# Stick-breaking attention in a two-layer decoder trunk: suffix sums by scans along rows in place of triangular matmuls

## The chip, the cores and the metric

One Trainium2 chip, one of its cores. The metric is the device time of one execution in microseconds (us). Three executions of the kernel before took 1234.39, 1236.29 and 1236.81 us, median 1236.29.

## What is computed

A trunk of two layers on x (512 tokens of 1024 channels, float32). Layer 0 has HGRN2 recurrence and forgetting attention, layer 1 a Griffin recurrent branch and stick-breaking attention with 8 heads of 64; each layer ends in an output projection, layer norms and a SwiGLU block. The change is in the stick-breaking attention:

```
z = einsum('bqhd,bkhd->bhqk', q, k) * 64 ** -0.5      # per block of 128 queries
mask = kpos < qpos
log_one_minus = where(mask, log_sigmoid(-z), 0)
suffix = cumsum(log_one_minus, axis=keys, reverse=True) - log_one_minus
w = where(mask, exp(log_sigmoid(z) + suffix), 0)
out = einsum('bhqk,bkhd->bqhd', w, v)
```

With softplus(z) = max(z, 0) + log(1 + exp(-|z|)), which is -log_sigmoid(-z), the exponent of w for one query is z minus the sum of softplus over this key and all later ones below the diagonal.

## The kernel before, in words

Every large product runs on TensorE (PE) in float32r with both operands split into a high and a low part, so that one product is three matmuls (`mm3`, L256 to L258). Weights come in chunks of 128x1024: SP issues the DMA into `ws`, ScalarE (ACT) casts the high part `wh` (L245), VectorE (DVE) subtracts to get the low part `wl` (L246); five such pairs of buffers exist. A projection `proj` is 24 matmuls of 512 columns into one of two PSUM banks "g"; the next but one projection has to wait until the bank is read.

Layer 1 (`layer1`) runs `griffin`, then the values (`values`), then four head pairs `sb_pair(hp)`; after the fourth, the first half of the output projection (`out_rows(yc, S_WO1)`, PE tile `po`) is emitted, so that its matmuls can stand between those of the fourth pair. A scheduler orders each engine's instructions by priorities; the engines then run them strictly in that order.

One pair, step by step. `qk_pair` projects q and k (tile `pj`) and writes, per head e, the high half of 64 rows and the low half of 64 rows of one tile (`qk`), the rest of k in `kz` (ACT L727, L734; DVE L730, L735, L736). The second ACT copy of k is ordered behind the first DVE read of the same bank. `sb_pair` then has **keys on the partitions**: for each key block j the scores of all later queries, 512-128j columns, packed into five tiles of 512 columns a pair. Per tile:

- PE: two matmuls and a bf16 mask matmul per block (L931 to L933) into a bank "s"; ACT copies it to `z` in SBUF (L935).
- softplus: DVE clamps at 41 (L936), ACT exp and log (L937, L938), DVE max with z (L939). ACT casts the high part `sh` (L941), DVE makes the low part `sl` (L942).
- sums over keys: since keys lie on partitions, PE sums them, by a triangular matrix `ntri` within a block and by a matrix of -1 `none` for every later block, each for `sh` and `sl` (L953, tile `cu`).
- DVE adds `cu` to `z` (L955), ACT takes exp in place (L956).

The weights then stand as the product with v wants them (L964, 16 matmuls into `po`, ordered behind the last exp).

Of the kernel before, what the change touches and what calls it, by code (L numbers as in the profile page):

```python
# [56 lines left out]
class Trunk:  # L57
    def __init__(self, tc, ctx, ins, out):
        self.tc, self.nc, self.out = tc, tc.nc, out
        self.ins = ins  # L60

        self.cp = ctx.enter_context(tc.tile_pool(name="cp", bufs=1))
        tile_ = lambda n, shape, dt=F32: setattr(self, n, self.cp.tile(shape, dt, name=n))
        tile_("par", [P, NPP])

        tile_("fill", [P, 64])
# [7 lines left out]
        tile_("ntri", [P, P], F32R)  # L74
        tile_("none", [P, P], F32R)
# [110 lines left out]

    def constants(self):
        nc, ins, ph, cp = self.nc, self.ins, self.ph, self.cp
        cst = self.sb.tile([P, 4, P], F32, tag="gb", bufs=1, name="cst")
# [6 lines left out]
        cp_(self.ntri, cst[:, 3, :])  # L196
        nc.gpsimd.tensor_scalar(self.none, cst[:, 3, :], 0.0, -1.0, ALU.mult, ALU.add)
# [516 lines left out]
    def qk_pair(self, iq, ik, low, high=None):  # L714

        nc = self.nc
        hv = (slice(0, 64), slice(64, P))
        if self.qk4:  # L720
# [12 lines left out]
        for e, d in enumerate(hv):
            nc.scalar.copy(ks[e][d], kp[d])  # L734
            nc.vector.tensor_copy(ks[e][hv[1 - e]], kp[d])  # L735
            nc.vector.tensor_tensor(low[e][d], kp[d], ks[e][d].bitcast(F32), ALU.subtract)  # L736
        return qs, ks

# [85 lines left out]
    def griffin(self, xr):  # L824
# [27 lines left out]
        for i in range(2):  # L852
            nc.scalar.dma_start(gw[i], self.ins["gw"][i])
        st = []
        for j in range(4):
            ps = xr[j]
            xp = self.sb.tile([P, T], F32, tag="act", bufs=16, name=self.nm("xp"))
# [12 lines left out]
            ig = self.t2k("ig", tag="sh")  # L870
# [4 lines left out]
        gts = []  # L875
        for j in range(4):
            ps = self.proj(S_GR + j)
            g = self.t2k("gt", tag="sl")
            A(g, ps, AF.Gelu_apprx_tanh)
            gi = self.newest()  # L880
            gts.append(g)
# [4 lines left out]
        for j in range(4):  # L886
# [25 lines left out]
    def sb_pair(self, hp, v):  # L912
# [3 lines left out]
        yh, yl = self.act("yh"), self.act("yl")  # L916
        po = self.bank("ho", "po")

        tiles = (((0, 3, 384), (0, 1, 0)), ((1, 3, 384), (1, 1, 0)), ((0, 2, 0), (1, 2, 256)), ((0, 0, 0),), ((1, 0, 0),))
        sp = {}  # L920
        for parts in tiles:
            z, l = self.t2k("z", tag="z"), self.t2k("l", tag="l")
            for e in (0, 1):
                mine = [p for p in parts if p[0] == e]
                if not mine:
                    continue
                ps = self.bank("s", "z")
                for _, j, o in mine:
                    n = T - j * P
                    b = slice(j * P, j * P + P)  # L930
                    nc.tensor.matmul(ps[:, o:o + n], k[e][:, b], q[e][:, j * P:T], start=True, stop=False)  # L931
                    nc.tensor.matmul(ps[:, o:o + n], self.kz[e][:, b], q[e][:, j * P:T], start=False, stop=False)
                    nc.tensor.matmul(ps[:, o:o + P], self.identb, self.sbmask, start=False, stop=True)  # L933
                c = slice(min(p[2] for p in mine), max(p[2] + T - p[1] * P for p in mine))
                nc.scalar.copy(z[:, c], ps[:, c])  # L935
            nc.vector.tensor_scalar(l, z, EXP_MAX, None, ALU.min)  # L936
            A(l, l, AF.Exp)  # L937
            A(l, l, AF.Ln, bias=self.one)  # L938
            nc.vector.tensor_tensor(l, l, z, ALU.max)  # L939
            sh, sl = self.t2k("sh", dt=F32R, tag="sh"), self.t2k("sl", dt=F32R, tag="sl")  # L940
            nc.scalar.copy(sh, l)  # L941
            nc.vector.tensor_tensor(sl, l, sh.bitcast(F32), ALU.subtract)  # L942
            for e, j, o in parts:
                sp[e, j] = (sh, sl, o)
            sp[parts] = z
        for ti, parts in enumerate(tiles):
            z = sp[parts]
            ps = self.bank(("pt", "po")[ti % 2], "cu")
            lo = [(self.none, sp[e, i], o + (i - j) * P, T - i * P) for e, j, o in parts for i in range(j + 1, NTB)]
            mms = [(self.ntri, sp[parts[0][:2]][:2] + (0,), 0, T)] + lo  # L950
            for n, (w, (sh, sl, oi), c, m) in enumerate(mms):
                for x in (sh, sl):
                    nc.tensor.matmul(ps[:, c:c + m], w, x[:, oi:oi + m], start=n == 0 and x is sh,  # L953
                                     stop=n == len(mms) - 1 and x is sl)
            nc.vector.tensor_tensor(z, z, ps, ALU.add)  # L955
            A(z, z, AF.Exp)  # L956
            ex = self.newest()

        at = {(e, j): (sp[parts], o) for parts in tiles for e, j, o in parts}
        for j in range(NTB):  # L960
            for e in range(2):
                h = 2 * hp + e
                z, o = at[e, j]
                nc.tensor.matmul(po[64 * e:64 * e + 64, j * P:T], v[j][:, h * 64:h * 64 + 64], z[:, o:o + T - j * P],  # L964
                                 start=j == 0, stop=j == NTB - 1)
                if j == 0 and e == 0:
                    self.behind(self.newest(), ex)
        self.put(po, yh, yl)
        return yh, yl

    def layer1(self, xr):
# [19 lines left out]
def hybrid_trunk_kernel(ctx: ExitStack, tc: tile.TileContext, out, **ins):  # L991
# [9 lines left out]
    with t.phase("l1", v=4, qk=7, kz=2, z=6, l=4, sh=5, sl=5) as t.ph:  # L1001
# [39 lines left out]
def layout(inp):  # L1041
# [70 lines left out]
```

## Time and profile before

| | us |
|---|---|
| runs, median of three | 1236.29 |
| the profiled execution's own time | 1234.76 |
| its span in the trace | 1233.0 |
| PE busy | 1211.3 (98%) |
| DVE busy | 760.3 (62%) |
| ACT busy | 522.0 (42%) |

The chain of work that ended last lies on PE for 90% of the span. A PE matmul row of 512 columns is 0.39 us long though the next starts 0.23 us later: ends are modelled, rows overlap, and so a short pause doesn't show as idle time. The engines' clock row shows the share of full speed that PE was granted.

### The profile page before, as it was taken

The page shows a single profiled execution, that of the slowest core. Times are in us where ns is not written, and L with a number is a line of the kernel's source. Part 1 is how long each engine was busy: PE and PEld are TensorE (multiplying, and loading weights), DVE is VectorE, ACT ScalarE, POOL GpSimd, SP SyncE. Part 2 cuts the span into 40 slices and gives each one's busy share as a digit, 9 for nine tenths or more (in the row PEclk, how much of TensorE's full clock was granted, in tenths as well). Part 3 has the DMA queues.
Part 4 walks back from the last instruction along what each step waited for, and adds up shares of the span by engine and source line. Part 5 has one row for each costly group of instructions (what it writes and reads, how often), then busy time and mean ns, then how long its engine had stood idle before and what let it go on. Part 6 is the DMA issues. An engine that isn't in the chain of part 4 may idle for free.

```text
span 1233.0 us, 15454 instructions
## 1 busy us (share of the span) xinstructions
PE 1211.3 (98%) x6119; PEld 985.0 (80%) x6119; DVE 760.3 (62%) x1157; ACT 522.0 (42%) x794; POOL 55.3 (4%) x81
## 2 busy tenths in 40 slices
PE   9999999999999999999999999999999999999997
PEld 7787777679888888878879776777988888888886
DVE  7638789768345635564387597686844554456346
ACT  7447567533333333332323757683333333333220
POOL 2000000000001000100000000000000100010001
PEclk9999999999999999999999998999999999999999
DMA  6421211134536433742324231102454642364321
GB/s 243 154 71 51 85 53 52 59 113 142 200 94 111 137 103 87 118 136 87 103 88 135 69 88 49 42 28 86 153 191 101 103 140 99 92 114 137 103 69 69
DMA packets 38727, 128.03 MB, mean 104 GB/s; under 512 B 4592, under 2 KB 6000, under 8 KB 38656
## 3 DMA queue, kind: packets, MB, share of 16 engines
q1 hardware_dynamic: 32496, 108.51, 27.5%
q0 software_dynamic: 4864, 16.81, 8.3%
q10 hardware_dynamic: 1296, 1.73, 0.4%
q8 instruction: 48, 0.79, 0.3%
q14 instruction: 23, 0.19, 0.0%
HBM read 124.90 MB, written 2.10 MB: 103 GB/s over the span
## 4 chain that ended last, share of the span: by engine, by line
PE 90%; DVE 5%; ACT 2%; DMA 1%; issue 1%; DVEq 0%; ACTq 0%
PE pf L257 13%; PE pf L256 13%; PE pf L258 13%; PE pj L256 5%; PE pj L257 5%; PE pj L258 5%; PE po L258 4%; PE po L256 4%; PE po L257 4%; PE fa L256 2%; PE fa L258 2%; PE fa L257 2%; PE sc L641 1%; PE pv L257 1%; PE pv L256 1%; PE pv L258 1%
## 5 line engine op out<-in xcount | busy, mean ns | idle before, releaser
L245 ACT CAST wh<-ws 128x1024 fp32r<-128x1024 f32 x143 | 150.2, 1051 | 308.8 <-PE pf L257 122.4
L246 DVE TENSOR_TENSOR wl<-ws,wh 128x1024 fp32r<-128x1024 f32 x143 | 174.9, 1223 | 155.9 <-ACT wh L245 151.2
L256 PE MATMUL pf<-xh,wh 128*128 128x512 f32 x640 | 249.0, 389 | 0.0
L257 PE MATMUL pf<-xl,wh 128*128 128x512 f32 x640 | 249.0, 389 | 0.0
L258 PE MATMUL pf<-xh,wl 128*128 128x512 f32 x640 | 249.0, 389 | 0.0
L258 PEld LDWEIGHTS pf<-xh,wl 128*128 128x128 f32 x640 | 120.2, 188 | 25.0
L257 PEld LDWEIGHTS pf<-xl,wh 128*128 128x128 f32 x640 | 120.2, 188 | 24.9
L256 PEld LDWEIGHTS pf<-xh,wh 128*128 128x128 f32 x640 | 120.2, 188 | 24.8
L531 DVE TENSOR_TENSOR s<-s,pf 128x512 f32<-128x512 f32 x44 | 30.3, 688 | 148.0 <-PE pf L258 148.0
L256 PE MATMUL pj<-xh,wh 128*128 128x512 f32 x256 | 104.3, 407 | 1.0 <-DVE qk L730 0.9
L258 PE MATMUL pj<-xh,wl 128*128 128x512 f32 x256 | 104.0, 406 | 0.0
L257 PE MATMUL pj<-xl,wh 128*128 128x512 f32 x256 | 103.8, 405 | 0.0
L251 ACT CAST wh<-wwah 128x1024 fp32r<-128x1024 f32 x32 | 33.7, 1054 | 74.3 <-PE pf L257 63.3
L256 PEld LDWEIGHTS pj<-xh,wh 128*128 128x128 f32 x256 | 48.6, 190 | 12.0 <-PE pj L258 1.7
L258 PEld LDWEIGHTS pj<-xh,wl 128*128 128x128 f32 x256 | 48.6, 190 | 10.2 <-issue 1.6
L257 PEld LDWEIGHTS pj<-xl,wh 128*128 128x128 f32 x256 | 48.6, 190 | 9.7 <-issue 1.1
L256 PE MATMUL fa<-wh,fm 128*128 128x512 f32 x128 | 49.9, 390 | 1.1 <-ACT wh L251 1.1
L256 PE MATMUL po<-wh,yh 128*128 128x512 f32 x128 | 50.9, 397 | 0.0
L258 PE MATMUL po<-wh,yl 128*128 128x512 f32 x128 | 50.6, 396 | 0.0
L257 PE MATMUL po<-wl,yh 128*128 128x512 f32 x128 | 50.3, 393 | 0.0
L252 DVE TENSOR_TENSOR wl<-wwah,wh 128x1024 fp32r<-128x1024 f32 x32 | 38.7, 1220 | 18.5 <-ACT wh L251 17.9
L257 PE MATMUL fa<-wl,fm 128*128 128x512 f32 x128 | 49.8, 389 | 0.0
(281 smaller groups left out, 2294.8 us busy)
## 6 DMA issues: line engine op xcount, KB each, us to landing
ws<-in_wst SPq DMA_DIRECT2D x165, 512.0 KB, 3.5
wwah<-in_wst POOLq DMA_DIRECT2D x24, 512.0 KB, 5.6
gb<-in_lnp SPq DMA_DIRECT2D x8, 512.0 KB, 4.6
wwah<-in_wst SPq DMA_DIRECT2D x8, 512.0 KB, 6.0
wwal<-in_wst SPq DMA_DIRECT2D x8, 512.0 KB, 6.9
wwal<-in_wst POOLq DMA_DIRECT2D x8, 512.0 KB, 6.4
ws<-in_wst SPq DMA_DIRECT2D x11, 256.0 KB, 5.2
xt<-in_xT SPq DMA_DIRECT2D x8, 256.0 KB, 5.3
```

Source lines behind the costliest of these rows:

```text
L245: nc.scalar.copy(hi, st)
L246: nc.vector.tensor_tensor(lo, st, hi.bitcast(F32), ALU.subtract)
L251: self.nc.scalar.copy(hi, dst)
L252: self.nc.vector.tensor_tensor(lo, dst, hi.bitcast(F32), ALU.subtract)
L256: mm(ps, ah, bh, start=first, stop=False, **kw)
L257: mm(ps, ah, bl, start=False, stop=False, **kw)
L258: mm(ps, al, bh, start=False, stop=last, **kw)
L531: nc.vector.tensor_tensor(h, h, pb, ALU.mult)
L641: nc.tensor.matmul(ps[u:u + 64, g * 256 + c * 64:g * 256 + (c + 1) * 64], E[:, c * P + u:c * P + u + 64], rhs, start=True, stop=True)
```

## The change

Now **queries are on the partitions** and keys along the row: per query block i and head there are 128(i+1) key columns, again five tiles of 512 columns a pair. Scores stay in their PSUM bank (three banks in turn: s, s, sc). Softplus is in split form: ACT takes |z| out of the bank, exp(-|z|), log(1 + .); DVE adds max(z, 0) from the bank. The sum over later keys is a DVE scan along the row read backwards; DVE subtracts it from the bank's z. PE transposes the difference, 128x128 at a time, into a bank, and ACT takes exp out of that bank into the tile `pT`, from which the product with v reads. `ntri` and `none` go (a filler tile grows by as much), and ACT instead of DVE makes the low copy of k. `griffin` keeps its four `ig` and `gt` tiles in two large ones of the `pT` slot.

```diff
@@ qk_pair
             nc.scalar.copy(ks[e][d], kp[d])
-            nc.vector.tensor_copy(ks[e][hv[1 - e]], kp[d])
+            (nc.vector.tensor_copy if self.qk4 else nc.scalar.copy)(ks[e][hv[1 - e]], kp[d])
@@ sb_pair
-        tiles = (((0, 3, 384), (0, 1, 0)), ((1, 3, 384), (1, 1, 0)), ((0, 2, 0), (1, 2, 256)), ((0, 0, 0),), ((1, 0, 0),))
...
+        tiles = (((0, 3, 0),), ((1, 3, 0),), ((0, 2, 0), (0, 0, 384)), ((1, 2, 0), (1, 0, 384)), ((0, 1, 0), (1, 1, 256)))
+        pT = self.t2k("pT", [P, 20 * P], tag="pT")
+        at = ((15, -6), (1, 5))
+        rev = lambda a: a[:, ::-1]
+        for ti, parts in enumerate(tiles):
+            tag = "zl"[ti % 2]
+            l = self.t2k("l", tag=tag)
+            ps = self.bank(("s", "s", "sc")[ti % 3], "z")
+            for e, i, o in parts:
+                n = (i + 1) * P
+                c = slice(i * P, n)
+                nc.tensor.matmul(ps[:, o:o + n], q[e][:, c], k[e][:, 0:n], start=True, stop=False)
+                nc.tensor.matmul(ps[:, o:o + n], q[e][:, c], self.kz[e][:, 0:n], start=False, stop=False)
+                nc.tensor.matmul(ps[:, o + i * P:o + n], self.identb, self.sbmask, start=False, stop=True)
+            A(l, ps, AF.Abs)
+            A(l, l, AF.Exp, scale=-1.0)
             A(l, l, AF.Ln, bias=self.one)
...
+            nc.vector.scalar_tensor_tensor(l, ps, 0.0, l, ALU.max, ALU.add)
+            for e, i, o in parts:
+                r = rev(l[:, o:o + (i + 1) * P])
+                nc.vector.tensor_tensor_scan(r, self.ones1[:, 0:(i + 1) * P], r, 0.0, ALU.mult, ALU.add)
+            nc.vector.tensor_tensor(l, ps, l, ALU.subtract)
+            pt = self.bank(("pt", "po")[ti % 2], "pt")
+            for e, i, o in parts:
+                b, step = at[e]
+                for j in range(i + 1):
+                    m = j if step > 0 else i - j
+                    nc.tensor.transpose(pt[:, o + m * P:o + (m + 1) * P], l[:, o + j * P:o + (j + 1) * P], self.ident)
+            for e, i, o in parts:
+                ...
+                A(dst, pt[:, o:o + (i + 1) * P].rearrange("p (j t) -> p j t", t=P), AF.Exp)
```

The scheduler moves instructions too. In the rows below, of the first pair, line numbers of the changed kernel are its own: L925 to L927 are the scores, L932, L935 and L936 softplus, scan and difference, L943 the transposes, L956 the product with v, L723 to L732 are `qk_pair`, L242 and L252 to L254 the weights' low part and the projections.

PE, first pair, between the second pair's k projection and the product with v. Before:

```order
L258 MATMUL pj_6228<-xh,wl_6225 128x512
L953 MATMUL cu_6124<-sh_6090,none 128x256
L953 MATMUL cu_6133<-sh_6090,none 128x256
L953 MATMUL cu_6124<-sl_6091,none 128x256
L953 MATMUL cu_6124<-sh_6052,none 128x128
L953 MATMUL cu_6124<-sl_6053,none 128x128
L953 MATMUL cu_6133<-sl_6091,none 128x256
```

Of the change:

```order
L943 MATMUL pt_6080<-ident,l_6065 128x128 x4
L254 MATMUL pj_6186<-xh,wl_6183 128x512
L252 MATMUL pj_6186<-xh,wh_6182 128x512
L253 MATMUL pj_6186<-xl,wh_6182 128x512
L254 MATMUL pj_6186<-xh,wl_6183 128x512
L943 MATMUL pt_6102<-ident,l_6087 128x128 x4
L252 MATMUL pj_6341<-xh,wh_6337 128x512
L925 MATMUL z_6222<-qk_6143,qk_6141 128x512
L925 MATMUL z_6256<-qk_6143,qk_6141 128x384
```

The last `cu` matmuls of a pair stood together with nothing between; the transposes stand in groups of four with projection matmuls and the next pair's scores between them.

DVE, first pair, at the same place. Before:

```order
L246 TENSOR_TENSOR wl_6858<-ws_6855,wh_6857 128x1024
L939 TENSOR_TENSOR l_6095<-l_6095,z_6094 128x512
L939 TENSOR_TENSOR l_6110<-l_6110,z_6109 128x512
L955 TENSOR_TENSOR z_6038<-z_6038,cu_6124 128x512
L942 TENSOR_TENSOR sl_6106<-l_6095,sh_6105 128x512
L942 TENSOR_TENSOR sl_6121<-l_6110,sh_6120 128x512
```

Of the change (the scan, L935, prints as SCALAR_TENSOR_TENSOR):

```order
L726 SCALAR_TENSOR_TENSOR qk_6141<-pj_6151,qk_6141 64x512
L936 TENSOR_TENSOR l_6087<-z_6088,l_6087 128x512
L242 TENSOR_TENSOR wl_6714<-ws_6711,wh_6713 128x1024
L932 SCALAR_TENSOR_TENSOR l_6109<-z_6110,l_6109 128x512
L726 SCALAR_TENSOR_TENSOR qk_6142<-pj_6151,qk_6142 64x512
L935 SCALAR_TENSOR_TENSOR l_6109<-ones_5507,l_6109 128x256 x2
L732 TENSOR_TENSOR kz_5503<-pj_6186,qk_6143 64x512
```

The read of the projection's bank (qk_6142, which frees it for pj_6341 above) now stands behind a weight chunk's subtraction and a softplus.

## Rows read from the trace of the kernel before

**Rows 1.** The page's first part: busy us, share of the span and instructions of PE and of its weight loads, DVE, ACT and POOL.
```profile
PE 1211.3 (98%) x6119; PEld 985.0 (80%) x6119; DVE 760.3 (62%) x1157; ACT 522.0 (42%) x794; POOL 55.3 (4%) x81
```
**Rows 2.** Windows: stretch in us, its length, busy us (and instructions) of PE, PE weight loads, DVE, ACT, POOL, then the granted PE clock, DMA share, GB/s.
```profile
722.10:859.10 137.00, 130.49 (x627) 99.77 (x626) 101.55 (x154) 87.66 (x147) 0.92 (x1) 0.98 0.21 66
235.00:240.00 5.00, 3.10 (x16) 2.44 (x16) 4.12 (x9) 1.32 (x6) 0.00 (x0) 1.00 0.31 105
753.00:756.00 3.00, 0.62 (x2) 0.50 (x2) 3.00 (x6) 2.95 (x6) 0.00 (x0) 0.76 0.36 104
756.00:759.00 3.00, 3.00 (x10) 2.51 (x9) 2.73 (x6) 1.66 (x3) 0.00 (x0) 0.50 0.18 71
759.00:762.00 3.00, 3.00 (x15) 2.81 (x15) 1.89 (x4) 1.21 (x2) 0.00 (x0) 0.61 0.00 0
```
**Rows 3.** PE in order of time: start, length, instruction, idle time before it and its releaser.
```profile
735.76 0.39 PE L257 MATMUL pj<-xl,wh 128*128 128x512 f32 x1
735.99 0.39 PE L258 MATMUL pj<-xh,wl 128*128 128x512 f32 x1
...
739.12 0.30 PE L932 MATMUL z<-qk,kz 128*128 128x128 f32 x1
739.26 0.23 PE L933 MATMUL z<-sbmask,identb 128*128 128x128 bf16 x1
739.29 0.42 PE L931 MATMUL z<-qk,qk 128*128 128x384 f32 x1
739.55 0.34 PE L932 MATMUL z<-qk,kz 128*128 128x384 f32 x1
...
755.49 0.80 PE L953 MATMUL cu<-sh,ntri 128*128 128x512 f32 x1 [2.38 <-DVE z L955]
...
762.81 2.95 PE L964 MATMUL po<-z,v 128*64 128x512 f32 x16
765.70 0.23 PE L933 MATMUL z<-sbmask,identb 128*128 128x128 bf16 x1
...
783.31 0.47 PE L953 MATMUL cu<-sh,ntri 128*128 128x512 f32 x1 [0.31 <-DVE z L955]
...
784.61 0.44 PE L256 MATMUL pj<-xh,wh 128*128 128x512 f32 x1
```
**Rows 4.** What PE waited for between 722 and 860 us: us in total, times, the longest.
```profile
PE cu L953 <- DVE z L955: 3.9, 6, 2.4
PE z L931 <- DVE qk L735: 1.0, 1, 1.0
PE pj L256 <- DVE qk L730: 0.9, 1, 0.9
```
**Rows 5.** The instructions of tile `cu`, high parts: count, duration in ns (min/median/max), first and last start, shapes. The low parts `sl` have as many.
```profile
L953 PE MATMUL cu<-sh,none x48: 220/280/522, 751.5 to 833.1; 128*128 128x128 f32 x24, 128*128 128x256 f32 x16, 128*128 128x384 f32 x8
L953 PE MATMUL cu<-sh,ntri x20: 389/468/797, 745.5 to 832.0; 128*128 128x512 f32 x20
```
**Rows 6.** PE in order of time, in layer 0's attention, where a group of four 128x128 float32 transposes (`pt`) stands among matmuls of 512 columns.
```profile
248.44 0.60 PE L788 MATMUL pt<-ident,p 128*128 128x128 f32 x4
248.79 0.48 PE L257 MATMUL po<-wl,yh 128*128 128x512 f32 x1
249.11 0.39 PE L258 MATMUL po<-wh,yl 128*128 128x512 f32 x1
```
**Rows 7.** ACT between 722 and 862 us, groups by line and shape: count, busy us, mean ns of one, idle us before and its releaser.
```profile
L938 ACT ACTIVATE l<-l,one 128x512 f32<-128x512 f32 x20 | 13.8, 718 | 0.0
L956 ACT ACTIVATE z<-z 128x512 f32<-128x512 f32 x20 | 12.3, 630 | 9.2 <-DVE z L955 9.2
L941 ACT CAST sh<-l 128x512 fp32r<-128x512 f32 x20 | 12.0, 617 | 0.5 <-DVE l L939 0.4
L937 ACT ACTIVATE l<-l 128x512 f32<-128x512 f32 x20 | 12.0, 628 | 2.1 <-DVE l L936 2.1
L935 ACT COPY z<-z 128x512 f32<-128x512 f32 x16 | 9.2, 584 | 1.1 <-PE z L933 1.0
L734 ACT CAST qk<-pj 64x512 fp32r<-64x512 f32 x8 | 4.6, 581 | 5.2 <-DVE kz L736 5.2
```
**Rows 8.** DVE between 722 and 862 us, groups in the same form.
```profile
L246 DVE TENSOR_TENSOR wl<-ws,wh 128x1024 fp32r<-128x1024 f32 x15 | 18.3, 1221 | 6.5 <-ACT wh L245 6.4
L942 DVE TENSOR_TENSOR sl<-l,sh 128x512 fp32r<-128x512 f32 x20 | 13.5, 685 | 0.9 <-ACT sh L941 0.9
L955 DVE TENSOR_TENSOR z<-z,cu 128x512 f32<-128x512 f32 x20 | 13.4, 682 | 3.5 <-PE cu L953 3.4
L936 DVE TENSOR_SCALAR l<-z 128x512 f32<-128x512 f32 x20 | 8.2, 423 | 2.5 <-ACT z L935 2.4
L735 DVE CAST qk<-pj 64x512 fp32r<-64x512 f32 x8 | 5.5, 689 | 1.5 <-ACT qk L734 1.3
L332 DVE SCALAR_TENSOR_TENSOR xt<-xt,po 128x512 f32<-128x512 f32 x8 | 5.5, 682 | 2.9 <-PE po L258 2.9
L904 DVE TENSOR_TENSOR_SCAN ig<-w,ig 128x512 f32<-128x512 f32 x1 | 1.2, 1225 | 0.0
```
**Rows 9.** DVE in order of time in layer 0: four scans of 128 columns, and an operation one of whose operands has a negative step.
```profile
25.58 1.37 DVE L567 TENSOR_TENSOR_SCAN bb<-ones,bb 128x128 f32<-128x128 f32 x4
...
28.59 0.68 DVE L629 TENSOR_TENSOR E<-bb 128x512 f32<-128x512 f32 x1
```

More of the change, by code (lines that the diff above doesn't have):

```diff
@@ L64, in __init__ @@
         tile_("par", [P, NPP])
-        tile_("fill", [P, 64])
+        tile_("fill", [P, 320])
         for n in ("one", "eps", "nhalf"):
@@ L73, in __init__ @@
             tile_(n, [P, P], BF16)
-        tile_("ntri", [P, P], F32R)
-        tile_("none", [P, P], F32R)
         self.sm = ctx.enter_context(tc.tile_pool(name="sm", bufs=1))
@@ L188, in constants @@
         nc, ins, ph, cp = self.nc, self.ins, self.ph, self.cp
-        cst = self.sb.tile([P, 4, P], F32, tag="gb", bufs=1, name="cst")
+        cst = self.sb.tile([P, 3, P], F32, tag="gb", bufs=1, name="cst")
         nc.sync.dma_start(cst, ins["cst"])
@@ L195, in constants @@
         cp_(self.sbmask, cst[:, 2, :])
-        cp_(self.ntri, cst[:, 3, :])
-        nc.gpsimd.tensor_scalar(self.none, cst[:, 3, :], 0.0, -1.0, ALU.mult, ALU.add)
         self.lvl = self.odd.tile([P, len(LEVELS), 64], U8, name="lvl")
@@ L854, in griffin @@
         st = []
+        igs, gts = [self.t2k("ig", [P, 20 * P], tag="pT") for _ in range(2)]
         for j in range(4):
@@ L869, in griffin @@
             A(r, pa, AF.Sigmoid, bias=par[:, C_BA + j:C_BA + j + 1])
-            ig = self.t2k("ig", tag="sh")
+            ig = igs[:, j * T:(j + 1) * T]
             A(ig, px, AF.Sigmoid, bias=par[:, C_BX + j:C_BX + j + 1])
@@ L874, in griffin @@
             st.append((r, ig))
-        gts = []
         for j in range(4):
             ps = self.proj(S_GR + j)
-            g = self.t2k("gt", tag="sl")
-            A(g, ps, AF.Gelu_apprx_tanh)
+            A(gts[:, j * T:(j + 1) * T], ps, AF.Gelu_apprx_tanh)
             gi = self.newest()
-            gts.append(g)
         with self.tc.issue_after(gi):
@@ L904, in griffin @@
             nc.vector.tensor_tensor_scan(ix, w, ix, 0.0, ALU.mult, ALU.add)
-            nc.vector.tensor_tensor(ix, ix, gts[j], ALU.mult)
+            nc.vector.tensor_tensor(ix, ix, gts[:, j * T:(j + 1) * T], ALU.mult)
             yh, yl = self.act("yh"), self.act("yl")
@@ L917, in sb_pair @@
         po = self.bank("ho", "po")
-        tiles = (((0, 3, 384), (0, 1, 0)), ((1, 3, 384), (1, 1, 0)), ((0, 2, 0), (1, 2, 256)), ((0, 0, 0),), ((1, 0, 0),))
[L920 to L937, printed above, removed]
-            A(l, l, AF.Ln, bias=self.one)
[L939 to L957, printed above, removed]
@@ L959, in sb_pair @@
-        at = {(e, j): (sp[parts], o) for parts in tiles for e, j, o in parts}
+        tiles = (((0, 3, 0),), ((1, 3, 0),), ((0, 2, 0), (0, 0, 384)), ((1, 2, 0), (1, 0, 384)), ((0, 1, 0), (1, 1, 256)))
[14 more added lines that the diff above has]
+            A(l, l, AF.Exp, scale=-1.0)
+            A(l, l, AF.Ln, bias=self.one)
+            nc.vector.scalar_tensor_tensor(l, ps, 0.0, l, ALU.max, ALU.add)
[10 more added lines that the diff above has]
+            for e, i, o in parts:
+                b, step = at[e]
+                lo = b + i + (0 if step > 0 else i * step)
+                dst = bass.AP(tensor=pT.tensor, offset=pT.offset + lo * P,
+                              ap=[pT.ap[0], [abs(step) * P, i + 1], [1, P]])
+                A(dst, pt[:, o:o + (i + 1) * P].rearrange("p (j t) -> p j t", t=P), AF.Exp)
@@ L960, in sb_pair @@
+        cp = self.newest()
         for j in range(NTB):
@@ L962, in sb_pair @@
                 h = 2 * hp + e
-                z, o = at[e, j]
-                nc.tensor.matmul(po[64 * e:64 * e + 64, j * P:T], v[j][:, h * 64:h * 64 + 64], z[:, o:o + T - j * P],
+                x = (at[e][0] + at[e][1] * j + j) * P
+                nc.tensor.matmul(po[64 * e:64 * e + 64, j * P:T], v[j][:, h * 64:h * 64 + 64], pT[:, x:x + T - j * P],
                                  start=j == 0, stop=j == NTB - 1)
                 if j == 0 and e == 0:
-                    self.behind(self.newest(), ex)
+                    self.behind(self.newest(), cp)
         self.put(po, yh, yl)
@@ L976, in layer1 @@
             self.nc.gpsimd.memset(self.kz[e][64 - 64 * e:P - 64 * e].bitcast(F32), 0.0)
+        self.ones1 = self.t2k("ones", tag="one")
+        self.nc.gpsimd.memset(self.ones1, 1.0)
         yc = self.griffin(xr)
@@ L1000, in hybrid_trunk_kernel @@
         xr = t.proj_halves(wa)
-    with t.phase("l1", v=4, qk=7, kz=2, z=6, l=4, sh=5, sl=5) as t.ph:
+    with t.phase("l1", v=4, qk=7, kz=2, z=5, l=4, pT=2, one=1) as t.ph:
         y = t.layer1(xr)
@@ L1081, in layout @@
     r = np.arange(P)
-    cst = np.zeros((P, 4, P), f)
+    cst = np.zeros((P, 3, P), f)
     cst[:, 0, :] = np.eye(P)
     cst[:, 1, :] = np.where(r[None, :] > r[:, None], -1e30, 0)
-    cst[:, 2, :] = np.where(r[:, None] >= r[None, :], -1e30, 0)
-    cst[:, 3, :] = np.where(r[:, None] >= r[None, :], -1, 0)
+    cst[:, 2, :] = np.where(r[None, :] >= r[:, None], -1e30, 0)
     o["cst"] = cst
```

## The prediction

> **What bounds the kernel now.** I read the page's busy shares first: PE is busy for 98% of the span, DVE for 62%, ACT for 42% [rows 1]. So the end is set by how much PE has to do and by its pauses, and only there can this change act. Next I cut out the one stage that it touches: from the first matmul of the first pair's q projection (722.1 us) to the first transposes of the layer norm (859.1), 137.0 us, with a PE clock of 0.98 and DVE busy 101.6 us, ACT 87.7 [rows 2]. All before it and behind it keeps its instructions, apart from two small POOL operations and 64 KB of a DMA in layer 0, off the path: nothing there.
>
> How much of the 137.0 us is work? By counting the order, 192 projection and 138 output-projection matmuls of 512 columns fall in it; such matmuls start 0.23 us apart (735.76, 735.99; 0.227 over longer runs) [rows 3], so 330 x 0.227 = 74.9. Scores: 4 pairs x 5120 columns at 0.227/512 us each = 9.1; 32 mask matmuls of some 0.04 = 1.3; and each mask costs twice some 0.08 where the type changes (the 384-column matmul at 739.29 holds the array until 739.55, 0.26 where 0.17 is its share, and the one ahead of the mask takes 0.14 for 0.06) [rows 3], 5.1. Products with v: 2.89 (762.81 to 765.70) [rows 3] x 4 = 11.6. Sums `cu`, below, 18.3. Together 120.2. The other **16.8 us are lost**: visible waits of 5.8 [rows 4], above all one of 2.38 us ahead of 755.49 [rows 3]; a fallen clock right after it, 0.50 and 0.61 in the two stretches behind [rows 2], which costs 3.00 x 0.50 + 3.00 x 0.39 and a little before, 3.0; and some 8 in pauses too short to show under modelled ends.
>
> **The change, part by part.** *Removed from PE:* 2 x 20 matmuls of 512 columns and 2 x (24 x 128 + 16 x 256 + 8 x 384) columns [rows 5], 40,960 columns x 0.227/512 = 18.2; the whole last tile of the second pair, 2560 columns, took 783.31 to 784.61, 1.30 [rows 3], which with its starts would make 20.8 for all. I take 18.3, since the starts are in the lost part.
>
> *Added to PE:* 80 transposes in 20 groups of four. In layer 0 such a group starts at 248.44, the next matmul at 248.79, and that one holds 0.32 instead of 0.23 [rows 6]: 0.35 + 0.09 = 0.44 a group, 8.8 in all; up to 0.54 a group if each waits for its semaphore, 10.8. Net work: **9.5 less**, between 7.4 and 12.0. Scores, masks and products with v keep their counts and widths.
>
> *ACT, per pair:* the five casts `sh` go (5 x 0.617), two copies of k come (2 x 0.581), |z| out of the bank costs what the copy to SBUF did (0.584), and exp out of the transposed bank is cut into eight pieces, some 0.3 more [rows 7]. 1.6 us less.
>
> *DVE, per pair:* the clamp (0.423), the max, the `sl` and the `cu` addition (0.68 each) and two copies of k (0.689) go: 5 x 2.47 + 1.4 = 13.8 [rows 8]. New are five additions of max(z,0) out of PSUM (0.682, as the addition of L332), five differences (0.682, as L955) [rows 8] and eight scans. A scan is dear: 1.225 for 512 columns [rows 8] where a sum is 0.68, and 0.34 for 128 (four in 1.37) [rows 9]; on the line between, 384 take 0.93 and 256 take 0.63. That makes 2 x (1.22 + 0.93 + 0.63 + 0.34) = 6.2, with the rest 13.1: about what goes. With the projections' reads, two weight chunks and the low part of the result a pair takes DVE 18.9 us; PE needs 10.9 + 3.9 + 2.2 + 2.9 = 19.9. So PE still has more to do, but only just, and the gain must be reduced by waits.
>
> *Waits.* Each tile now runs scores, three ACT steps (0.58 + 0.63 + 0.72), three DVE steps (0.68 + 1.22 + 0.68), transposes, exp. In the first pair I went along the orders with these lengths. PE waits some 1.2 for k (before: 1.0 [rows 4]), 0.5 for the first difference; then it has 12 projection matmuls and the fourth tile's scores (3.6 us) while DVE must do a weight chunk 1.22, two additions 1.36, scans 1.22 + 0.93 and a difference 0.68 = 5.4: a wait of 1.4; 0.3 at the third group; at the fourth, DVE 2.6 (scans 1.27, bank read 0.69, difference 0.68) against PE's 1.4: 1.2. Then the next projection needs its bank, whose read stands behind a weight chunk and an addition: 2.6 against 0.45, a wait of 2.1, the longest. The last group and the exps ahead of the product: 0.8 + 0.5. Sum 8.0, and 7 since DVE's rows overlap their neighbours. In the later pairs more matmuls of other work stand between the groups (18, 7, 7 and 6 in the second, 16, 8, 14 and 7 in the third, the output projection in the fourth); the same count gives 1.9, 1.1 and 1.0. With the 0.9 at the very start that stays [rows 4] it is 11.9, and of the pauses too short to see I leave 3, because the 40 `cu` dependencies on casts and subtractions are replaced by 20 on differences. **Lost after: 14.9**, 1.9 less than before.
>
> Sum: 9.5 + 1.9 = 11.4 us. Against the profiled execution's own 1234.76 us (span 1233.0) that is 1223.4; that execution was 1.53 us below the median of 1236.29, from which I count: **1225.0 us**.
>
> **The bounds.** Lost as little as 8.4 (half the first pair's waits, no short ones) gives a gain of 17.9: 1218.4. If all 16.8 stay lost, the transposes take 10.8 and the clock falls once more for 3.0, the gain is 7.5 - 3.0 = 4.5: 1231.8.
>
> **The rivals.** *The clock.* [...] One fall in the first pair is well possible and gives 1228, inside the range. One in each pair costs 4 x 3.0 = 12.0: 1237.0, no change. [...]
>
> *The scan read backwards.* No scan in this trace has a negative step; the nearest row is an addition of which one operand steps back between its halves, 0.68 [rows 9], like any other. If backward scans took twice the forward time, DVE would need 25.1 us a pair, 5.2 more than PE, in three pairs (the fourth has the output projection as cover): 15.6. If that takes the place of all the 10.0 us of waits of these pairs, 20.5 are lost; if the first pair's 7 come on top, 27.5. The gain is then 5.8 to -1.2, in the middle 2.3, which is no change: 1234.0. [...]
>
> *Every pair waits as the first does.* This ends slower. Its place is the order of PE: if ACT and DVE fall behind, by the casts `wh` and the subtractions `wl` that are put ahead of the softplus steps, the 18 or 16 matmuls of cover are used up while DVE still works. Its price is 7 us in each of the three later pairs in place of 4.0 together: 17 more lost, 1242. It decides from (11.4 + 4.0)/3 = 5.1 us of waits a pair on. For it speaks that DVE and PE have almost the same to do; against it, that before DVE had as much to do (19.6 a pair) and PE still waited only 5.8 us in all [rows 4].
>
> **How the numbers follow.** Forecast with its bounds, one clock fall included: 0.84. Clock falls in each pair 0.05, backward scan 0.05, every pair waits 0.06. Less than 0.2% (2.5 us), about what a measurement of this kernel can tell, is no change. Faster by more: nearly all of the forecast, 0.83 (between 1231.8 and 1233.8 a thin end), and 0.02 of the rivals, where they come out weaker: 0.85. No change: 0.09, from the first two rivals. Slower: 0.06, the third. The range runs from 1218.5 to 1232.0; the rivals beyond it hold 0.16.
>
> **What the profile of the changed kernel would show.** Right: the stage from the first pair's q projection to the first `tr` takes 125 to 126 us; no row `cu`; 80 rows `pt<-ident,l`, a group of four some 0.44; scans near 1.22 at 512 columns; PE clock 1.00 in the first pair; PE waits on DVE's difference and once on `qk`, some 7 us in the first pair and 1 to 2 in each later one. Wrong: scans above 2 us; a stretch at 0.5 after the wait for the projection's bank; waits of 5 us or more in the second and third pair; or a stage as long as before with fewer matmuls in it, which would say that the sums along partitions were hidden work, as no row here does.

## The result, and the profile after

The changed kernel takes **1222.58 us** (median of four runs, 1221.4 to 1224.0) where the kernel before takes 1236.38 (four executions too): ratio 0.9895, 95% interval 0.9881 to 0.9909. The forecast was 1225.0, the range 1218.5 to 1232.0. The profiled execution took 1224.0 us, its span 1222.0, 11.0 less than before.

The page's first part, after; against [rows 1] PE has 14.4 us less, and is as full as before:

```profile
PE 1196.9 (98%) x6063; PEld 970.9 (79%) x6063; DVE 757.4 (62%) x1141; ACT 517.9 (42%) x790; POOL 54.8 (4%) x80
```

Windows after, columns as in [rows 2]: the stage (first matmul of the first pair's q projection to the first `tr`), the stretch at 235 us, three stretches in the first pair, and all behind the stage:

```profile
722.50:847.00 124.50, 114.12 (x571) 85.60 (x570) 98.75 (x138) 83.46 (x143) 0.99 (x1) 0.99 0.23 72
235.00:240.00 5.00, 2.96 (x13) 2.25 (x13) 4.38 (x8) 1.36 (x6) 0.00 (x0) 0.84 0.40 105
757.00:758.00 1.00, 0.43 (x1) 0.29 (x1) 0.97 (x2) 0.97 (x2) 0.00 (x0) 0.59 0.85 131
758.00:760.00 2.00, 2.00 (x6) 1.67 (x6) 1.97 (x4) 0.43 (x1) 0.00 (x0) 0.50 0.48 195
760.00:761.00 1.00, 1.00 (x6) 0.60 (x4) 0.35 (x2) 0.74 (x2) 0.00 (x0) 0.70 0.00 0
847.00:1222.00 375.00, 366.59 (x1718) 306.65 (x1718) 199.60 (x267) 113.33 (x143) 20.44 (x23) 0.99 0.42 113
```

The stage went from 137.0 to **124.5 us**, 12.5 less. The granted clock still fell to 0.50 once in the first pair, from 757.2 to 760.6 us, where before it stood at 0.50 from 754.5 to 761.4. Behind the stage 375.0 us stand against 373.9, and ahead of it 0.4 more, so that 11.0 of the 12.5 reach the end.

PE in order of time in the first pair, after, with what it waited for:

```profile
738.17 0.68 PE L925 MATMUL z<-qk,qk 128*128 128x512 f32 x2 [1.12 <-ACT qk L731]
...
745.74 0.66 PE L943 MATMUL pt<-ident,l 128*128 128x128 f32 x4 [0.35 <-DVE l L936]
746.16 0.42 PE L925 MATMUL z<-qk,qk 128*128 128x384 f32 x1
...
750.64 0.65 PE L943 MATMUL pt<-ident,l 128*128 128x128 f32 x4 [0.69 <-DVE l L936]
...
752.32 0.60 PE L943 MATMUL pt<-ident,l 128*128 128x128 f32 x4
752.67 0.48 PE L254 MATMUL pj<-xh,wl 128*128 128x512 f32 x1
...
754.86 0.63 PE L943 MATMUL pt<-ident,l 128*128 128x128 f32 x4 [1.01 <-ACT wh L241]
757.57 0.79 PE L252 MATMUL pj<-xh,wh 128*128 128x512 f32 x1 [2.09 <-DVE qk L726]
```

No `cu` is left. A group of four transposes holds PE for 0.42 us before the next matmul starts when it comes out of a wait (745.74), and for 0.35 us without one (752.32). The longest wait, 2.09 us, is the one for the projection's bank, and the clock fell in the course of it. PE's waits in the whole stage, after (us in total, times, longest), to be read beside [rows 4]:

```profile
PE pt L943 <- DVE l L936: 4.6, 9, 0.8
PE pj L252 <- DVE qk L726: 3.3, 2, 2.1
PE z L925 <- ACT qk L731: 1.1, 1, 1.1
PE pt L943 <- ACT wh L241: 1.0, 1, 1.0
PE pt L943 <- ACT l L929: 0.2, 1, 0.2
```

DVE in the stage, after, groups as in [rows 8]:

```profile
L936 DVE TENSOR_TENSOR l<-z,l 128x512 f32<-128x512 f32 x20 | 13.6, 683 | 0.3
L932 DVE SCALAR_TENSOR_TENSOR l<-z,l 128x512 f32<-128x512 f32 x20 | 13.3, 682 | 8.2 <-ACT l L931 8.2
L935 DVE TENSOR_TENSOR_SCAN l<-ones,l 128x512 f32<-128x512 f32 x8 | 9.6, 1216 | 0.2
L935 DVE TENSOR_TENSOR_SCAN l<-ones,l 128x384 f32<-128x384 f32 x8 | 7.6, 944 | 0.0
L935 DVE TENSOR_TENSOR_SCAN l<-ones,l 128x256 f32<-128x256 f32 x8 | 5.1, 676 | 0.1
L935 DVE TENSOR_TENSOR_SCAN l<-ones,l 128x128 f32<-128x128 f32 x8 | 3.2, 405 | 0.0
```

The backward scan costs what a forward one does: 1216 ns for 512 columns beside 1225.

### The profile page after: what moved, and what is told of

It is laid out like the page before. It is cut to its first block, busy times and chain, and to the rows that moved or that the text cites. A ratio compares the mean times of both kernels' runs of the same rounds, so it can differ in the third digit from the quotient of the medians.

```text
span 1222.0 us, 15335 instructions
## 1 busy us (share of the span) xinstructions
PE 1196.9 (98%) x6063; PEld 970.9 (79%) x6063; DVE 757.4 (62%) x1141; ACT 517.9 (42%) x790; POOL 54.8 (4%) x80
## 4 chain that ended last, share of the span: by engine, by line
PE 86%; DVE 7%; ACT 3%; DMA 3%; issue 1%; SPq 0%; DVEq 0%; ACTq 0%
PE pf L253 13%; PE pf L252 13%; PE pf L254 13%; PE pj L252 4%; PE pj L253 4%; PE pj L254 4%; PE po L254 4%; PE po L253 4%; PE po L252 4%; PE fa L252 2%; PE fa L253 2%; PE fa L254 2%; DMA ws<-in_wst 2%; PE sc L637 1%; DVE l L935 1%
## 5 line engine op out<-in xcount | busy, mean ns | idle before, releaser
L242 DVE TENSOR_TENSOR wl<-ws,wh 128x1024 fp32r<-128x1024 f32 x143 | 174.8, 1223 | 151.9 <-ACT wh L241 148.5
L252 PE MATMUL pf<-xh,wh 128*128 128x512 f32 x640 | 249.0, 389 | 0.0
L254 PE MATMUL pf<-xh,wl 128*128 128x512 f32 x640 | 249.0, 389 | 0.0
L254 PEld LDWEIGHTS pf<-xh,wl 128*128 128x128 f32 x640 | 120.1, 188 | 25.1
L252 PEld LDWEIGHTS pf<-xh,wh 128*128 128x128 f32 x640 | 120.1, 188 | 24.9
L252 PE MATMUL pj<-xh,wh 128*128 128x512 f32 x256 | 104.6, 409 | 3.6 <-DVE qk L726 3.3
L254 PE MATMUL pj<-xh,wl 128*128 128x512 f32 x256 | 104.1, 407 | 0.0
L252 PEld LDWEIGHTS pj<-xh,wh 128*128 128x128 f32 x256 | 48.6, 190 | 15.7 <-issue 3.0
L254 PEld LDWEIGHTS pj<-xh,wl 128*128 128x128 f32 x256 | 48.5, 190 | 10.2 <-issue 1.6
L252 PE MATMUL po<-wh,yh 128*128 128x512 f32 x128 | 51.6, 403 | 0.0
L254 PE MATMUL po<-wh,yl 128*128 128x512 f32 x128 | 51.0, 398 | 0.0
L252 PE MATMUL fa<-wh,fm 128*128 128x512 f32 x128 | 50.0, 390 | 0.7 <-ACT wh L247 0.7
L248 DVE TENSOR_TENSOR wl<-wwah,wh 128x1024 fp32r<-128x1024 f32 x32 | 38.7, 1221 | 18.5 <-ACT wh L247 17.9
L254 PE MATMUL fa<-wh,fm 128*128 128x512 f32 x128 | 49.8, 389 | 0.0
```

The source lines that it names most:

```text
L242: nc.vector.tensor_tensor(lo, st, hi.bitcast(F32), ALU.subtract)
L248: self.nc.vector.tensor_tensor(lo, dst, hi.bitcast(F32), ALU.subtract)
L252: mm(ps, ah, bh, start=first, stop=False, **kw)
L254: mm(ps, al, bh, start=False, stop=last, **kw)
```

## The experiments

To read them I split each stage of a profile into three: PE's busy time times what the granted clock lacked there to 1.00 (what the clock cost), the waits that the trace shows (0.15 us and more; all of them, so that before has 6.4 where the three lines of [rows 4] make 5.8), and the rest, which is PE's work with the shorter pauses. Clock and waits are those of one profiled execution each; the medians are of all executions.

| kernel | median us | ratio to before (95%) | stage | clock | waits | rest |
|---|---|---|---|---|---|---|
| before | 1236.4 | | 137.0 | 2.9 | 6.4 | 127.7 |
| changed | 1222.6 | 0.9895 (0.9881 to 0.9909) | 124.5 | 1.5 | 10.2 | 112.8 |
| e1, before, high sums only | 1228.0 | 0.9939 (0.9924 to 0.9955) | 129.8 | 3.0 | 10.5 | 116.2 |
| e2, transposes twice | 1228.8 | 0.9942 (0.9927 to 0.9957) | 130.5 | 0.0 | 8.1 | 122.4 |
| e3, k copies on DVE | 1224.9 | 0.9912 (0.9898 to 0.9927) | 126.7 | 2.8 | 10.4 | 113.5 |
| e4, scans twice | 1251.7 | 1.0126 (1.0109 to 1.0144) | 151.3 | 10.7 | 29.0 | 111.6 |
| e5, before, k copies on ACT | 1232.9 | 0.9982 (0.9972 to 0.9991) | 133.9 | 0.0 | 6.0 | 127.9 |
| e9, max(z,0) on ACT | 1227.0 | 0.9932 (0.9920 to 0.9945) | 128.6 | 2.9 | 12.8 | 113.0 |
| e12, bank read ahead | 1221.7 | 0.9886 (0.9869 to 0.9902) | 121.9 | 0.0 | 7.8 | 114.1 |
| e14, mask in fp32r | 1225.3 | 0.9912 (0.9898 to 0.9926) | 126.8 | 0.0 | 13.1 | 113.7 |

The last column stands within 111.6 to 114.1 for every kernel that has the changed kernel's PE work, give or take the masks' type, in whatever order and with whatever waits; the other two columns hold what the order decides and, since each is one execution, some chance.

**e1: half of the sums' work out of the kernel before.**

```diff
-                for x in (sh, sl):
+                for x in (sh,):
...
```

> The kernel before, with only the high halves of softplus in the `cu` sums: the low halves' 20 x 512 columns and the rest, 20,480 columns in all, are left out (the result loses their precision; the subtraction that makes the low halves still runs on DVE). Work theory: PE is what counts and its matmuls come off nearly one for one. 20,480 x 0.227/512 = 9.1 us less, of which waits for DVE's additions may take back up to 3: 1227 to 1230 where the kernel before has 1236.4. Rival, the chain theory: the stage is as long as its chain of ACT and DVE steps, the change gained by taking casts, subtractions and additions out of it, and the sums along partitions are hidden work: less than 2.5 us, 1234 to 1237.

0.9939, some 7.5 us less: the work theory, and the chain theory falls. The rest falls by 11.5, more than the columns' 9.1, so the 68 matmuls had some 2.4 us of starts and short pauses of their own; 4.1 of the 11.5 came back as waits for DVE and ACT.

**e2: twice the transposes.**

```diff
-                    nc.tensor.transpose(pt[:, o + m * P:...
+                    for _ in range(2):
+                        nc.tensor.transpose(pt[:, o + m * P:...
```

> The changed kernel with each of the 80 transposes of the softplus difference issued twice into the same place of its bank. A group of four took 0.36 from its start to the next matmul's, so 20 x 0.36 = 7.2 us of PE work are added. Work theory: +4 to +7.2 us, since DVE gets ahead meanwhile and some of the 5.8 us that PE now waits for DVE and ACT ahead of these groups goes: 1226.6 to 1229.8. Chain theory: PE has room ahead of its groups, less than +2.5: 1222 to 1225.

0.9942 against 0.9895: +5.8 us, the work theory again. The rest rises by 9.6, 0.48 a group; 2.1 of waits and the half clock (1.5) went in exchange.

**e3 and e5: the copies of k alone.** e3 undoes that part of the change, e5 makes it alone in the kernel before.

```diff
-            (nc.vector.tensor_copy if self.qk4 else nc.scalar.copy)(ks[e][hv[1 - e]], kp[d])
+            nc.vector.tensor_copy(ks[e][hv[1 - e]], kp[d])
```

> The changed kernel with the two copies of k per pair back on DVE. DVE gets 2 x 0.689 = 1.4 us more per pair, ACT 1.2 less. If DVE's margin to PE (18.9 against 19.9 us a pair in the prediction's count) is what keeps the waits small, PE waits about 1.4 more in two or three of the pairs: +1.5 to +4, 1224 to 1226.6. Rival: ACT's chain is as tight, and the copies only change which engine is late: -1 to +1, 1221.5 to 1223.6.

> The kernel before with one part of the change alone: the two copies of k per pair go from DVE to ACT. DVE has 1.4 us less a pair. If PE's waits come from DVE, some of the 3.9 us that it waits for DVE's additions in this stage goes, and with the 2.38 us wait perhaps the half clock behind it, which cost 3.4 us of TensorE time: -1 to -6 against 1235.4, 1229.5 to 1234.5. Rival, that this part carries nothing of the gain: -1 to +1, 1234.4 to 1236.4.

e3 has 1224.9, within the first theory's 1224 to 1226.6, but not for its reason: waits of 10.4 beside 10.2, and 2.8 of half clock where the changed kernel has 1.5. e5 gains 2.2 us, again with nearly as many waits (6.0 beside 6.4: those for DVE's additions fell from 3.9 to 1.7, but 2.5 for ACT's copies of k stand where 1.0 stood for DVE's): its profile loses the half clock. Windows of e5 where the kernel before ran at half [rows 2]:

```profile
754.00:756.00 2.00, 1.56 (x11) 1.33 (x12) 1.96 (x3) 1.96 (x4) 0.00 (x0) 1.00 0.02 4
756.00:759.00 3.00, 1.65 (x12) 1.42 (x11) 2.76 (x5) 2.95 (x6) 0.00 (x0) 1.00 0.45 160
```

Its longest wait is 1.4 us, where before had 2.4. So this part alone, in the kernel before, is worth some 2 us (e5's interval); for e3 it is an indication only, since its interval overlaps the changed kernel's. That it works through the clock is not shown: each is one profile, and over all executions the granted clock averages 0.9954 in e5 and 0.9948 before, which is worth some 0.7 us of the 2.2, and 0.9955 both in e3 and in the changed kernel.

**e4: a DVE that falls behind.** Each scan runs twice.

```diff
-                nc.vector.tensor_tensor_scan(r, self.ones1[...], r, 0.0, ALU.mult, ALU.add)
+                for _ in range(2):
+                    nc.vector.tensor_tensor_scan(r, self.ones1[...], r, 0.0, ALU.mult, ALU.add)
```

> The changed kernel with each of the eight scans per pair run twice on the same row (the sums are then sums of sums). DVE gets 6.2 us more a pair, 25 against PE's 20 to 22: the case of the prediction's second rival. By that rival's count 20.5 to 27.5 us are lost in place of the 14.9 forecast: +6 to +13, 1228.5 to 1235.5. If PE's waits do not depend on DVE (the scans beside other work in all pairs): less than +2.5, 1222 to 1225.

1251.7, +29 where 6 to 13 were expected: the mechanism holds, the size does not. PE's longest waits in e4's stage, and windows of it:

```profile
PE pt L944 <- DVE l L937: 17.1, 12, 3.1
PE pj L252 <- DVE qk L726: 4.3, 2, 3.1
PE z L925 <- DVE wl L242: 3.0, 1, 3.0
```

```profile
756.00:771.00 15.00, 8.19 (x31) 5.45 (x33) 12.95 (x21) 7.43 (x15) 0.00 (x0) 0.54 0.11 35
794.00:802.00 8.00, 5.49 (x18) 3.21 (x20) 4.40 (x7) 2.85 (x6) 0.00 (x0) 0.57 0.23 68
825.00:829.00 4.00, 4.00 (x13) 1.49 (x13) 1.65 (x3) 1.82 (x4) 0.00 (x0) 0.57 0.41 131
838.00:846.00 8.00, 6.22 (x25) 5.57 (x26) 7.32 (x12) 4.03 (x7) 0.00 (x0) 0.57 0.00 1
```

The waits are 29.0, where the upper count of the prediction's second rival, 27.5, has 24.5 of waits and 3 of short pauses; PE's clock fell four times, once in each pair, and cost 10.7 on top, and in this profile another 3 us were lost ahead of the stage, whose code is the same. The rivals on DVE and on the clock, priced apart in the prediction, come together: in e4 PE waits for DVE in every pair and its granted clock falls to 0.50 in every pair, each time in, or just behind, a stretch of some 2 to 3 us in which PE stood still (in windows of 1 us: 754 to 757, 793 to 797, 820 to 824 and 836 to 840). In the stage of the changed kernel there is one fall, in e2, e12 and e14 none, with as many groups of transposes in these banks.

**e9: less for DVE, more for ACT.** `x` is `m` read backwards like `r`.

```diff
-            nc.vector.scalar_tensor_tensor(l, ps, 0.0, l, ALU.max, ALU.add)
+            m = self.t2k("m", tag="one")
+            A(m, ps, AF.Relu)
...
-                nc.vector.tensor_tensor_scan(r, self.ones1[...], r, 0.0, ALU.mult, ALU.add)
+                nc.vector.tensor_tensor_scan(r, r, x, 0.0, ALU.add, ALU.add)
```

> The changed kernel with max(z,0) taken by ACT out of the bank (Relu, some 0.58 each) and added inside the scan, which then sums both operands; the addition on DVE (0.683 each, five a pair) is gone, 3.4 us a pair, and ACT has 2.9 more. Theory that DVE is the late engine: most of the 4.6 us of waits for DVE's difference goes, and perhaps the wait for the projection's bank and the half clock: -3 to -7 against 1222.6, 1215.5 to 1219.5. Rival: ACT, busy 18.5 of the third pair's 22 us now, is late in its place: 0 to +4, 1222.5 to 1226.5.

1227.0, slower than the changed kernel: my theory that DVE alone is late is wrong here, and the rival holds, 0.5 us beyond its range. DVE's busy time fell from 98.75 to 88.14 us, yet its own waits for ACT's logarithm rose from 8.2 us (the row of L932 above) to 15.4, here from e9's waits of DVE:

```profile
DVE l L936 <- ACT l L931: 15.4, 11, 2.1
```

and PE waited 4.5 us once at a group in the first pair. So in the changed kernel ACT and DVE are probably both nearly as tight as PE, and work moved from one to the other changes which of them is late. That is not the only reading: the edit also takes one of the five buffers of tag `z` for `m`, and fewer buffers alone were not tried.

**e7, e10, e11, e13: more cover for the first pair.** The first pair's projections are written ahead of the values' projection (e7), with e9's edit (e10), with the first score held in PE's order behind the values' last matmul, `lastpv` (e11), and with the bank's reads of e12 as well (e13).

```diff
+        qk0 = self.qk_pair(S_QD, S_KD, self.kz)
         v = self.values(S_VD)
...
-            yd.append(self.sb_pair(hp, v))
+            yd.append(self.sb_pair(hp, v, qk0 if hp == 0 else None))
```

```diff
                 nc.tensor.matmul(ps[:, o:o + n], q[e][:, c], k[e][:, 0:n], start=True, stop=False)
+                if qk:
+                    self.behind(self.newest(), self.lastpv)
```

> The changed kernel with the first pair's q and k projections written ahead of the values' projection, so that the next pair's projections stand as cover between the first pair's groups. Theory: the first pair's waits (1.1 for k, 0.35, 0.69, 1.01 and 2.1, 5.3 in all) and the half clock behind the last, 1.7 us, are lost for want of cover; most of it goes, -3 to -7 against 1222.6: 1215.5 to 1219.5. Rival: DVE has so little margin that the waits turn up in later pairs instead: -1.5 to +1.5, 1221 to 1224.

> Both edits together, the first pair's projections ahead of the values' and max(z,0) on ACT. Of the stage's 13.8 us that are not PE work (10.2 visible waits, 1.7 half clock, 1.9 short) some 7 to 10 go if cover and DVE are what is short: 1212.5 to 1216. If ACT is late in their place, no better than the projections ahead alone: 1217 to 1222.

> The kernel with the first pair's projections ahead of the values', its first score now held behind the values' last matmul in PE's order. In the run without that, PE stood 18.4 us at that score, which waited for ACT's copy of k, and the clock was at half for another 3.3 us behind it, 1.7 us of work. Theory: the cover does what it was meant to once PE does not stand there: 1237.4 - 18.4 - 1.7 = 1217.3, between 1215 and 1219.5. Rival: the first pair's waits only move to later pairs: 1221 to 1224.

All three miss their forecasts and are slower than even the kernel before: 1237.4 (ratio 1.0021, 1.0012 to 1.0030), 1241.9 (1.0055, 1.0043 to 1.0068) and 1237.5 (1.0016, 1.0007 to 1.0025). PE in e7 stands once for 18.4 us, in e10 too:

```profile
729.39 0.80 PE L925 MATMUL z<-qk,qk 128*128 128x512 f32 x1 [18.37 <-ACT qk L731]
```

From this row I put the first score behind the values. In e11 PE stands as long, now at the values:

```profile
730.38 0.77 PE L252 MATMUL pv<-wh,xh 128*128 128x512 f32 x1 [18.42 <-DVE qk L727]
```

DVE in e11, in order of time, shows why:

```profile
727.06 0.68 DVE L897 TENSOR_TENSOR ig<-ig,w 128x512 f32<-128x512 f32 x1
727.77 0.68 DVE L727 SCALAR_TENSOR_TENSOR qk<-pj,qk 64x512 fp32r<-64x512 f32 x1
728.49 0.69 DVE L248 TENSOR_TENSOR yl<-ig,yh 128x512 fp32r<-128x512 f32 x1
729.10 0.42 DVE L898 TENSOR_SCALAR w<-w 128x512 f32<-128x512 f32 x1
729.55 0.69 DVE L727 SCALAR_TENSOR_TENSOR qk<-pj,qk 64x512 fp32r<-64x512 f32 x1
```

Up to here DVE works off the recurrence (`griffin`); the reads of q's projection (L727) stand behind most of it, and until the second is done, at 730.24, the values have no bank. The values' matmuls had been the cover of the recurrence. The wait that e7 named was only the last of two with nearly the same end: there too the second of these reads ends at 729.30, and PE starts at 729.39. e13 puts those reads ahead:

> Both edits of order together, the first pair's projections ahead with its score held behind the values, and the bank's reads ahead on DVE. If they act on different waits: 1214 to 1217.5. If the projections ahead alone already take the first pair's waits, as much as that run alone, within 1.5.

1222.4 (0.9902, 0.9887 to 0.9917): 15 us better than e11, which shows the cause of those 18 us, and no better than the changed kernel, 5 us short of the forecast. Its profile has no half clock in the first pair, but waits of 2.0 us for a group of transposes and 2.6, in two, for the values' copies.

**e12: the bank's reads ahead on DVE, alone.**

```diff
+            with self.tc.high_priority(offset=1 if self.qk4 else 700):
                 nc.vector.scalar_tensor_tensor(qs[e][hv[1 - e]], qp[d], 0.125, ...
```

> The changed kernel with DVE's two reads of the q projection's bank put ahead of the weight chunk and the softplus additions that stood in front of them. Theory: the wait of 2.1 us for the projection's bank in the first pair and the half clock behind it (1.7) go: -2 to -4, 1218.6 to 1220.6. Rival: the softplus steps then come as much later and PE waits for DVE's difference instead: -1 to +1.5, 1221.6 to 1224.

The stage does what the theory says: 121.9 us, 2.6 less, without the wait of 2.1 and without half clock (over its four executions the granted clock averages 0.9970 against 0.9955). The end does not: 1221.7, with an interval that overlaps the changed kernel's. In this profile 377.6 us follow the stage in place of 375.0. One weight transfer of the last stage, in the chain of waits of e12 and then of the changed kernel (start, length):

```profile
1086.42 10.09 DMA wwal<-in_wst
```

```profile
1088.41 8.41 DMA wwal<-in_wst
```

It was issued 2 us earlier and landed 0.3 us earlier, and PE waited 3.1 us in all for such weights' casts (`fa <- ACT wh`), 0.7 in the changed kernel, none before. Whether coming earlier makes this transfer longer or it merely varies was not tried, and stays open; the profiled execution was the slowest of four, of which the fastest took 1217.7.

**e14: a term of the sum by itself.** The mask and its identity are kept in fp32r.

```diff
-                nc.tensor.matmul(ps[:, o + i * P:o + n], self.identb, self.sbmask, start=False, stop=True)
+                nc.tensor.matmul(ps[:, o + i * P:o + n], self.identr, self.sbmask, start=False, stop=True)
```

> The changed kernel with the mask and its identity kept in the fp32r type of the score matmuls instead of bf16. It tests a term of the sum, 5.1 us for 32 masks with a change of type on either side, some 0.08 each, and it may beat both kernels. If the term is right, 32 x (0.16 - 0.02 for the wider type) = 4.5 us of PE work go, of which four fifths came through when matmuls were taken out before: -2 to -4.5 against 1222.6, 1218 to 1220.6. Rival: the 0.08 belong to the narrow matmul and not to the change of type, or the waits take it back: -1 to +2, 1221.6 to 1224.6.

1225.3, no gain and above both ranges. PE around a mask in the changed kernel, then in e14:

```profile
739.38 0.23 PE L927 MATMUL z<-sbmask,identb 128*128 128x128 bf16 x1
739.42 0.42 PE L926 MATMUL z<-kz,qk 128*128 128x384 f32 x1
739.68 0.23 PE L927 MATMUL z<-sbmask,identb 128*128 128x128 bf16 x1
739.72 0.31 PE L925 MATMUL z<-qk,qk 128*128 128x128 f32 x1
...
746.41 0.34 PE L926 MATMUL z<-kz,qk 128*128 128x384 f32 x1
746.59 0.23 PE L927 MATMUL z<-sbmask,identb 128*128 128x128 bf16 x1
```

```profile
740.07 0.22 PE L930 MATMUL z<-sbmask,identr 128*128 128x128 f32 x1
740.13 0.39 PE L929 MATMUL z<-kz,qk 128*128 128x384 f32 x1
740.36 0.22 PE L930 MATMUL z<-sbmask,identr 128*128 128x128 f32 x1
740.42 0.27 PE L928 MATMUL z<-qk,qk 128*128 128x128 f32 x1
```

The matmul of 384 columns right behind a mask (739.42, 740.13) holds PE for 0.23 us in place of 0.26, the mask itself for 0.06 in place of 0.04. So of the 0.09 above the 384 columns' share (0.17) only 0.03 came with the change of type, and the wider type takes it back. Ahead of a mask next to nothing is lost: the same matmul at 746.41, which has none before it, holds PE for 0.18. The order came out another way, and waits rose to 13.1.

No version here is shown to beat the changed kernel.

## Why the prediction was right, step by step

**What bounds the stage** was right: e1 and e2 took PE work out and put it in, and 7.5 and 5.8 us of the end went with it.

**Work.** The prediction counted 120.2 + 8 of short pauses before and 110.7 + 3 after: 128.2 and 113.7. The rest column has 127.7 and 112.8. The parts are not that good: half of `cu` is 11.5 us by e1, so that all of it would be some 23 rather than 18.3, beyond even the upper bound of 20.8. The trace of before says the same: from start to next start, without waits and with the half clock taken out, its 136 `cu` matmuls hold PE for 23.5 us. Some 3.9 us of PE's time above the columns' share lies on the 48 matmuls right behind a `cu` of 128 columns, as in the second pair before (the row between is 784.61 in [rows 3]):

```profile
784.44 0.23 PE L953 MATMUL cu<-sh,none 128*128 128x128 f32 x1
784.50 0.27 PE L953 MATMUL cu<-sl,none 128*128 128x128 f32 x1
...
784.89 0.39 PE L257 MATMUL pj<-xl,wh 128*128 128x512 f32 x1
```

Behind 256 columns the first holds PE for 0.06 us; behind 128 columns the second takes 0.11 for the same 128 columns and the projection 0.28 in place of 0.23. The transposes are 9.6 by e2, within 8.8 to 10.8; the 0.54 for a group that waits, behind the 10.8, was the author's estimate and no run shows it: out of a wait the group at 745.74 holds PE for 0.42 us and the matmul behind it for 0.08 more than its columns (746.16 to 746.41), 0.50. The net is then 13.4 in place of 9.5, and of the 5 us fewer short pauses, which were put down to fewer dependencies, 1.5 are left. Most of the short pauses belonged to the `cu` matmuls; the sum held because what one term lacked the other had. The 5.1 for masks was read wrongly: the loss falls once per mask, on the matmul behind it, and makes some 3 us, only a third of it from the change of type (e14). That changes nothing in the forecast, since the masks stay.

**ACT and DVE** were right to a few per cent in sum, as with 6.5 us of scans a pair for 6.2: rows of 1216, 944, 676 and 405 ns for the estimates of 1.22, 0.93, 0.63 and 0.34 us (the shortest a fifth more), addition and difference 682 and 683. ACT's exp in pieces of 512, 384, 256 and 128 columns takes 598, 490, 382 and 271 ns, two of each a pair: 0.33 us more than five of 630, for the 0.3 of the prediction.

**Waits.** Forecast 11.9 visible, measured 10.2; before had 6.4, not the 5.8 that the prediction took from the three longest lines. First pair: 1.2, 0.5, 1.4, 0.3, 1.2, 2.1, 0.8 + 0.5 were named; 1.12, 0.35, 0.69, none, 1.01, 2.09 and none came, 5.3 where 7 was forecast. The later pairs have 1.1, 1.6 and 1.0 for 1.9, 1.1 and 1.0. That the projection's bank would be the longest wait, and which engine ends each, came out by following the orders with row lengths. Two ends were shared with ACT: the fourth group's wait is put down to ACT's `wh`, which ends at 754.73, and DVE's difference ends at 754.71; and DVE's read of the bank itself waited 0.23 us for ACT's.

**The clock.** The forecast named a clock of 1.00 in the first pair as a sign of being right and a stretch at 0.5 after the wait for the projection's bank as a sign of being wrong, and kept one fall inside the range. That very stretch came: one fall, in a wait of 2.09 us, which cost 1.5; before, one in a wait of 2.38 us cost 2.9. So that step failed; that it cost little was luck, since e3, with the same wait of 2.09 us, lost 2.8. The rival with a fall in each pair did not come, but e4 shows that it is real once DVE is late: four falls, 10.7 us. A stretch without a fall in one profile is weak evidence against it: at 235 to 240 us the clock stayed at 1.00 before [rows 2], and the changed kernel, whose code is the same there, has 0.84.

**The scan read backwards** costs nothing extra: 1216 ns for 512 float32 columns, in place, beside 1225 forward. **Every pair waits** did not come: no later pair has more than 1.6 us of waits. With DVE made late, in e4, the waits are 29 us.

**What was left out**: 1.5 of the 12.5 us are given back outside the stage. 0.7 is a wait in the last stage for weights that now come later than PE, and 0.4 lies ahead of it, where this profile's clock fell and that of before did not.

**The sum.** Of the stage's gain the forecast 11.4 was 9.5 of work, 5 of short pauses and 3.0 of clock, less 6.1 of added waits. Measured, 12.5 is 13.4 of work, 1.5, 1.4, less 3.8. The path (PE's work comes off, waits for DVE take part of it back) was right; that the sum is so close owes something to errors of 3.9 and 3.5 us that cancel. Against the forecast stage of 125 to 126 us the real one is 0.5 to 1.5 better, and the end 2.4 better than 1225.0, within the runs' own spread of 2.6.

## What to carry to other kernels

When PE is full, price an edit by the PE work that it removes and adds, and take a work term from a stretch that contains its own starts and pauses, as here the whole 1.30 us tile rather than the columns alone (20.8 and 18.2 us for all of `cu`, where some 23 were measured). Then follow the in-order queues with measured lengths to find the waits: their sum came out within 1.7 us of 11.9. Before removing a wait by name, look what else ends at the same time, and before moving work ahead, what it covered: in e7 and e11 PE stood 18 us, in e11 for a bank whose reads stood behind other work.

## What the runs showed of the hardware that was not expected

- The same instructions ran at 1.00 of the clock in one execution (235 to 240 us before) and at 0.84 in the other, that of the changed kernel, which was at half from 238.4 to 241.8. In the stage the changed kernel was at half for 757.2 to 760.6, e3 for 755.7 to 762.5, both from within a wait of 2.09 us, while e13 waited 1.96 us at a group without a fall. An edit near such a point can be worth 1.5 to 3 us either way in one profile for reasons that its own work does not show.
- A matmul right behind a narrow one holds PE longer than its columns: by 0.05 us behind a `cu` of 128 columns, by 0.09 behind a bf16 mask of 128 or the last of four transposes (784.50, 739.42 and 752.67 in the rows above).
- A scan of 512 float32 columns takes 1216 ns with a negative step, 1221 with two data operands that are both added (e9), 1225 forward with multiply and add (L904 in [rows 8]): nearly the same.
